# Reordering TensorE in a kernel's second listing pass, and a new order of work in its opening

The case is a two-layer decoder trunk that runs on all 8 cores of one Trainium2 chip, one sequence of the batch per core. The metric is the device time of the slowest core, in microseconds.

## The reference, cut to what matters

```python
# x: (8, 2048, 1024) float32, c: (8, 1024); DEPTH 2, D_FF 2816
def modulate(x, g, mod):
    shift, scale, gate = jnp.split(mod, 3, axis=-1)
    h = rmsnorm(x, g) * (1.0 + scale[:, None, :]) + shift[:, None, :]
    return h, gate[:, None, :]

def swiglu(h, w_in, w_out):
    g, u = jnp.split(h @ w_in, 2, axis=-1)
    return (jax.nn.silu(g) * u) @ w_out

for l in range(DEPTH):
    mod = silu(c) @ w_mod[l] + b_mod[l]             # (8, 9*1024)
    mod_f1, mod_mx, mod_f2 = jnp.split(mod, 3, axis=-1)
    h, gate = modulate(x, norm_g[l, 0], mod_f1)
    x = x + 0.5 * gate * swiglu(h, w_ffn_in[l, 0], w_ffn_out[l, 0])
    # ... token mixer (l = 0: gating and short conv; l = 1: causal pooling), then a second SwiGLU
return rmsnorm(x, final_g)
```

Before the first weight matmul the kernel needs the first two tiles of x, their norms, and the shift and scale of layer 0: 16 "rows" of 128 modulation values, each a product of 512 KB of weights with the conditioning vector.

## The kernel before

The program is a list of operations with their data dependencies. A first pass places each operation in a model of the engines' time as the code adds it. A second pass (`relist`) runs the list again in that model: the engines named in `free` take, of the operations that are ready, the one with the earliest due date; all other engines keep the order of the first pass. The order that comes out is fixed in the program: each engine is given its own list.

```python
    def relist(self, free=("dve", "act")):
        ...
            due.append(o.start + (0.0 if o.eng == "pe" else 8.0))
        # due dates are pulled earlier where a successor needs it
        ...
        fixed = {e: [] for e in self.ENGS if e not in free}     # order of the first pass
        ...
                elif e in ready:
                    _, x = heapq.heappop(ready[e])              # free engine: earliest due date
                else:
                    if at[e] >= len(fixed[e]) or not isready[fixed[e][at[e]]]:
                        continue                                # fixed engine: waits for its next
                    x = fixed[e][at[e]]
```

The opening loads six rows, two tiles of x, then the other ten rows. Chunk c (128 of the 1024 columns) needs row c (shift) and row 8 + c (scale). "Row n" below is the n-th in order of use, 2k for the shift and 2k + 1 for the scale of the k-th chunk. A row is a chain of one-column f32 matmuls or one multiply-and-sum on VectorE:

```python
    order0 = [0, 4, 1, 5, 2, 6, 3, 7]
    on_pe = (0, 2, 4, 6, 8, 10, 12, 14, 15)
    ...
            if n in on_pe:
                b = banks0.next()                               # PSUM banks 0 and 1
                for kc in range(NC):
                    add("pe", I("matmul", PS[b][:, 0:1], ap[:, kc * 128:(kc + 1) * 128], CT[:, kc:kc + 1], ...
            else:
                stt(ap, ap, 1.0, CB[:], ALU.mult, ALU.mult, ..., accum_out=M)
    ...
    for s, k in zip(range(NSLOT), (3, 5, 6, 7, 7, 7)):          # six weight slots, 1 MB read each
        load_next(s, [("MOD", 0, order0[k])])                   # slot s waits for the k-th shift row
```

A SwiGLU unit then makes seven products of four 128x128x512 matmuls (P1 to P7) from one slot. The second half of x is loaded inside the first channel mixer:

```python
    def late_x():
        for t in range(2, 4):
            add("sp", I("dma_start", out=X[:, t, :, :], ...), reads=[("A", ablk(6, 0))], ...)   # 2 MB each
    ...
                    run_segs(segs[:X_AT])
                    late_x()
                    bg_add(stats_gen([2, 3]))                   # sums of squares of the two tiles
```

Such sums of squares (`ps<-SQ,ONES` in the profile) and the pooling products of layer 1 (`ps<-CB,WMOD`) are side jobs: small groups of matmuls put between the weight matmuls (`ps<-H,SLOTS` and `ps<-ACTB,SLOTS`).

## Time and profile before

| | before |
|---|---|
| time, median of 3 runs | 1972.81 us (1972.31 to 1972.99) |
| profiled run, slowest core | 1967.0 us |
| first weight matmul, median of the cores | 58.7 us |
| cores 2 to 7 / cores 0 and 1 | 1961.1 to 1967.0 / 1938.9 and 1943.3 us |

Six cores spent 151 to 154 us at a granted clock of 0.8125, two cores none, and the two groups lie 23 us apart (means 1964.3 and 1941.1 us). I call it the limiter.

In the opening most cores are granted only 0.5, on core 0 of this run for example from 42.0 to 62.4 us; but from 38.5 to 42.0 us that core had 1.0, and there 32 one-column matmuls of the rows, all but the last two started in that time, took

```profile
38.76 3.90 PE L463 MATMUL ps<-CT,ACTB 128*128 128x1 f32 x32
```

where the same 32 take 6.83 us on core 3 in the prediction below. Start to start that is 112 ns at 1.0 and 213 ns at 0.5: a row on TensorE takes 1.8 us or 3.4 us. The records of core 3 begin only at 61.8 us; the 1.00 that the prediction's views show before it stands for missing records.

Lines with an arrow in brackets give the idle time of the engine just before that group and what ended it. The prediction below shows the views of this kernel.

### The profile page before, as it was taken

Reading aid. Unit: us, or ns where it says so; the run is one execution under the profiler, and the core shown is the slowest. Engines: PE = TensorE matmul, PEld = TensorE weight load, DVE = VectorE, ACT = ScalarE, POOL = GpSimd, SP = SyncE. Lnnn points to the kernel's source line nnn. Section 1 sums busy time; section 2 is a strip of 40 time slices with the busy share of each in tenths; the row PEclk is TensorE's granted clock in tenths of the full one; section 3 lists DMA queues with packets and bytes.
Section 4 is the critical chain, followed back from the end, with each engine's and each line's share of the span. In section 5 each row is a group of like instructions: output and inputs, shape, how many; then the busy total and the mean of one; then the engine's idle time right before and its main releaser. Section 6 shows DMA issues by size and latency. Waiting matters only on the chain.

```text
span 1967.0 us, 25441 instructions; the slowest of 8 cores (1938.9 to 1967.0 us)
## 1 busy us (share of the span) xinstructions
PE 1920.7 (98%) x8750; PEld 874.8 (44%) x8750; DVE 1695.3 (86%) x3246; ACT 1032.8 (53%) x1738; POOL 172.2 (9%) x330
## 2 busy tenths in 40 slices
PE   6999999999999999999999999999999999999997
PEld 4533444444444444444444444444444444444443
DVE  3867899999798999999988888898998889888865
ACT  4443555455564655465455545564456555574343
POOL 0000000000202000000000000000000000000000
PEclk9887899999999999999999999999999999999998
DMA  9875668786777777776755554555454444445752
GB/s 283 164 186 121 135 130 171 172 171 138 158 161 173 162 152 172 157 154 135 169 105 86 86 86 85 87 97 86 76 86 70 84 84 86 75 75 86 173 87 95
DMA packets 66653, 248.72 MB, mean 126 GB/s; under 512 B 7520, under 2 KB 7648, under 8 KB 66016
## 3 DMA queue, kind: packets, MB, share of 16 engines
q0 software_dynamic: 42192, 153.64, 47.5%
q1 hardware_dynamic: 24336, 93.45, 14.4%
q8 instruction: 74, 1.21, 0.2%
q14 instruction: 51, 0.42, 0.1%
HBM read 392.29 MB, written 8.39 MB: 204 GB/s over the span
## 4 chain that ended last, share of the span: by engine, by line
PE 91%; DMA 4%; DVE 3%; ACT 1%; SPq 0%; issue 0%; DVEq 0%; POOLq 0%
PE ps L463 91%; DMA ACTB<-wmod 2%; DMA SLOTS<-wout 2%; DVE ACTB L463 1%; DVE SLOTS L463 1%; DVE X L463 0%; DVE WMOD L463 0%; SPq L463 0%; ACT PMH L463 0%; DVE TP L463 0%; ACT ps L463 0%; DVE ps L463 0%; ACT TP L463 0%; ACT L463 0%; ACT ACTB L463 0%
## 5 line engine op out<-in xcount | busy, mean ns | idle before, releaser
L463 PE MATMUL ps<-H,SLOTS 128*128 128x512 f16 x5440 | 1215.7, 383 | 6.6 <-ACT ps L463 2.2
L463 PEld LDWEIGHTS ps<-H,SLOTS 128*128 128x128 f16 x5440 | 534.9, 99 | 668.8 <-issue 83.7
L463 ACT ACTIVATE ps<-ps 128x512 f32<-128x512 f32 x684 | 398.0, 582 | 584.8 <-PE ps L463 548.6
L463 PE MATMUL ps<-ACTB,SLOTS 128*128 128x512 f16 x2780 | 622.5, 383 | 1.4 <-DVE TP L463 0.8
L463 PEld LDWEIGHTS ps<-ACTB,SLOTS 128*128 128x128 f16 x2780 | 273.7, 99 | 337.5 <-issue 30.6
L463 DVE TENSOR_TENSOR SLOTS<-SLOTS 128x512 f16<-128x512 f16 x996 | 395.2, 418 | 17.1 <-DMA SLOTS<-wout 8.0
L463 DVE SCALAR_TENSOR_TENSOR X<-ps,GH,X 128x512 f32<-128x512 f32 x424 | 308.3, 746 | 44.6 <-PE ps L463 37.6
L463 ACT ACTIVATE TP<-ps 128x512 f32<-128x512 f32 x400 | 238.0, 595 | 130.8 <-PE ps L463 130.5
L463 DVE TENSOR_TENSOR ACTB<-TP,ps 128x512 f16<-128x512 f32 x368 | 249.3, 684 | 46.4 <-PE ps L463 27.8
L463 ACT ACTIVATE SQ<-X 128x512 bf16<-128x512 f32 x224 | 131.4, 621 | 113.1 <-DVE X L463 57.9
L463 POOL DMA_DIRECT2D SLOTS<-win x176 | 93.1, 530 | 1046.0 <-PE ps L463 974.0
L463 DVE TENSOR_TENSOR TP<-ps,TP 128x512 f32<-128x512 f32 x176 | 121.2, 688 | 65.2 <-ACT ps L463 63.4
L463 DVE SCALAR_TENSOR_TENSOR WMOD<-WMOD,CB 128x1024 f32<-128x1024 f32 x129 | 156.8, 1218 | 2.8 <-DMA WMOD<-wmod 2.6
L463 DVE TENSOR_TENSOR TP<-X,RS 128x512 f32<-128x512 f32 x192 | 129.7, 686 | 12.5 <-ACT ACTB L463 8.5
L463 DVE TENSOR_TENSOR ps<-ps,TP 128x512 f32<-128x512 f32 x176 | 122.4, 696 | 15.2 <-PE ps L463 14.0
L463 DVE TENSOR_TENSOR ACTB<-ACTB 128x1024 f16<-128x1024 f16 (+1 forms) x188 | 104.6, 566 | 1.5
L463 POOL DMA_DIRECT2D SLOTS<-wout x88 | 46.5, 528 | 521.4 <-PE ps L463 521.4
L463 ACT ACTIVATE H<-TP,MODT,AS 128x512 f16<-128x512 f32 x81 | 62.7, 805 | 20.0 <-DVE TP L463 11.9
L463 PE MATMUL ps<-SQ,ONES 128*128 128x512 bf16 x130 | 44.7, 432 | 15.0 <-DVE SQ L463 6.7
L463 ACT ACTIVATE PMH<-TP,MODT,AS 128x512 f16<-128x512 f32 x60 | 47.6, 806 | 18.1 <-DVE TP L463 18.1
L463 ACT ACTIVATE ACTB<-TP,MODT,AS 128x512 f16<-128x512 f32 x51 | 40.8, 806 | 15.4 <-PE ps L463 12.5
L463 DVE TENSOR_TENSOR SQ<-SQ 128x1024 bf16<-128x1024 bf16 (+1 forms) x56 | 36.3, 649 | 12.2 <-ACT SQ L463 11.8
(74 smaller groups left out, 562.0 us busy)
## 6 DMA issues: line engine op xcount, KB each, us to landing
SLOTS<-win POOLq DMA_DIRECT2D x176, 512.0 KB, 6.0
WMOD<-wmod SPq DMA_DIRECT2D x131, 512.0 KB, 5.8
SLOTS<-wout POOLq DMA_DIRECT2D x88, 512.0 KB, 5.4
SLOTS<-wab POOLq DMA_DIRECT2D x28, 512.0 KB, 8.7
X<-xT SPq DMA_DIRECT2D x4, 2048.0 KB, 20.8
outT<-X SPq DMA_DIRECT2D x16, 512.0 KB, 3.7
ACTB<-wmod SPq DMA_DIRECT2D x13, 512.0 KB, 25.1
CB<-cb SPq DMA_DIRECT2D x1, 512.0 KB, 5.5
```

The lines of the kernel that those rows point to most:

```text
L463: return lambda E: getattr(E, name)(*a, **k)
```

## The change

The intent: let a ready matmul on TensorE overtake a waiting one, and let the opening start sooner. Whole, without context lines:

```diff
-X_AT = 60
+X_AT = 55
+SLG = (2, 3, 4, 6, 7, 7)
...
-    order0 = [0, 4, 1, 5, 2, 6, 3, 7]
-    on_pe = (0, 2, 4, 6, 8, 10, 12, 14, 15)
+    order0 = list(range(NC))
+    on_pe = (10, 12, 14, 15)
...
                 apply_chunk(0, 0, 0, order0[j], 1, HH)
-                if j % 2 == 1:
-                    h_sums(j // 2, 1)
         apply_chunk(0, 0, 0, order0[k], 0, HH)
         apply_chunk(0, 0, 0, order0[k], 1, HH)
-        if k % 2 == 1:
-            h_sums(k // 2, 1)
+        h_sums(k - 4, 1)
...
-    for s, k in zip(range(NSLOT), (3, 5, 6, 7, 7, 7)):
+    for s, k in zip(range(NSLOT), SLG):
         load_next(s, [("MOD", 0, order0[k])])
...
-    Sd.relist()
+    Sd.relist(("dve", "act", "pe"))
```

## The prediction

> **What bounds the kernel now.** I read the page first, then the cores, then a table of stretches, then TensorE alone in the stretches that were short of matmuls, then the opening's chain of waits.
>
> The page, its busy row and two of its rows of slices:
>
> ```profile
> span 1967.0 us, 25441 instructions; the slowest of 8 cores (1938.9 to 1967.0 us)
> PE 1920.7 (98%) x8750; PEld 874.8 (44%) x8750; DVE 1695.3 (86%) x3246; ACT 1032.8 (53%) x1738; POOL 172.2 (9%) x330
> PE   6999999999999999999999999999999999999997
> PEclk9887899999999999999999999999999999999998
> ```
>
> TensorE is busy 98% of the span. Only the first and last slices are not nearly full, and the clock row dips in slices 2 to 5. So the question is where TensorE loses time, and the table of stretches says:
>
> ```profile
> 0.00:10.00 10.00, 3.62 (x9) 1.12 (x9) 1.36 (x24) 2.55 (x3) 0.19 (x4) 1.00 0.74 167
> 50.00:60.00 10.00, 9.60 (x45) 8.99 (x45) 9.21 (x26) 4.70 (x7) 2.12 (x4) 1.00 0.96 177
> 100.00:150.00 50.00, 46.14 (x176) 18.58 (x174) 33.77 (x67) 24.68 (x44) 3.54 (x7) 0.81 0.78 180
> 150.00:200.00 50.00, 47.47 (x175) 19.23 (x174) 38.50 (x74) 16.57 (x28) 2.64 (x5) 0.77 0.51 124
> 1050.00:1100.00 50.00, 50.00 (x232) 22.51 (x231) 44.41 (x83) 29.52 (x51) 4.23 (x8) 1.00 0.47 78
> ```
>
> The columns are stretch, PE, PEld, DVE, ACT, POOL busy with counts, granted clock, DMA share, GB/s. An undisturbed stretch holds 232 matmuls in 50 us, 215 ns each: that is the bound, and no change of order beats it. At a clock of 0.81 a stretch holds only 175.
>
> The losses on the slowest core, from the matmuls' start times: the first matmul of the first channel mixer starts at 59.96 us; from there to 240 us the starts are 36 us further apart in all than 216 ns each would make them, nearly all of it the clock of 0.81 and a bubble near 150 us; from 240 us to the end of the matmuls only 15.7 us, in 36 places; after the last weight matmul some 13 us remain for the final norm and the output. The change can touch the 60 us in front, the bubble, and those 15.7 us.
>
> The opening, TensorE alone:
>
> ```profile
> 39.45 6.83 PE L463 MATMUL ps<-CT,ACTB 128*128 128x1 f32 x32
> 48.38 3.55 PE L463 MATMUL ps<-CT,ACTB 128*128 128x1 f32 x16 [2.10 <-DMA ACTB<-wmod]
> 51.79 3.55 PE L463 MATMUL ps<-CT,WMOD 128*128 128x1 f32 x16
> 55.20 3.55 PE L463 MATMUL ps<-CT,ACTB 128*128 128x1 f32 x16
> 59.16 1.01 PE L463 MATMUL ps<-SQ,ONES 128*128 128x512 bf16 x2 [0.40 <-DVE AS L463]
> 59.96 2.38 PE L463 MATMUL ps<-H,SLOTS 128*128 128x512 f16 x6
> ```
>
> The opening ends in three modulation rows done on TensorE one after the other (rows 12, 14 and 15 of 16), 3.4 us from start to start, and the first of them waited for its transfer. The chain of waits names that transfer for 29.48 us, issue to landing. DMA share is 0.96 to 1.02 from 10 to 60 us: the front is a full queue and then three serial rows.
>
> The late stalls, TensorE alone again:
>
> ```profile
> 147.20 0.70 PE L463 MATMUL ps<-SQ,ONES 128*128 128x512 bf16 x2
> 149.69 0.68 PE L463 MATMUL ps<-SQ,ONES 128*128 128x512 bf16 x2 [1.80 <-DVE SQ L463]
> 152.91 1.01 PE L463 MATMUL ps<-SQ,ONES 128*128 128x512 bf16 x2 [2.53 <-DVE SQ L463]
> ...
> 1456.24 0.98 PE L463 MATMUL ps<-CB,WMOD 128*128 128x512 f16 x3 [0.85 <-DVE CB L463]
> 1483.39 0.98 PE L463 MATMUL ps<-CB,WMOD 128*128 128x512 f16 x3 [1.78 <-DVE CB L463]
> 1699.75 0.38 PE L463 MATMUL ps<-CB,WMOD 128*128 128x512 f16 x1 [0.66 <-DVE CB L463]
> ```
>
> Here TensorE stands at the head of a side job (sums of squares, pooling products) while weight matmuls of the main stream lie behind it in its fixed order. This is just what reordering TensorE in the second pass is for.
>
> **What the Trainium skill says.** "TensorE: Matmul & The Clock Gate", section "Back-to-back issue gap", gives N/2.4 + 2.5 ns for a warm matmul, 216 ns at 512 columns; this trace has 215. Its section "The HAM clock gate" says an idle window of some 3.4 us halves the clock; the records agree, one piece of 6.8 us at 0.5 follows the bubble near 150 us (the stretch from 153 to 160 us holds 21 matmuls, where 0.81 would give 27). The same section says that three busy cores of a die bring the clock to 13/16 and that it is held while the load lasts: the trace shows 0.8125 on cores 2 to 7, but only from 69 to 229 us here, under an unchanged load, and on cores 0 and 1 not at all. So I take it as a fixed cost of about 160 x (1 - 0.8125) = 30 us on the slow cores, which the change does not touch. "DMA: Bandwidth & Descriptors", section "Queues, rings and completion order", says that an engine takes turns between queues packet by packet. The trace agrees: with slot 0's load in flight (37.06 to 48.20 us, 11 us for 1 MB read) the modulation rows land 1.3 to 4.6 us apart.
>
> **The change part by part.**
>
> (1) *TensorE in the second pass.* Nothing is added or removed; a ready matmul may now overtake a waiting one, in the pass's own model of time. Movable are the stalls at side jobs: 1.80 + 2.53 near 150 us, and 0.85 + 1.78 + 0.35 + 0.66 + 0.58 from 1455 to 1705 us (the 0.35 and 0.58 are sums of squares there), together 8.55 us. The cold piece goes too if the bubble falls below a window: 6.8 us x (1 - 0.5/0.8125) = 2.6 us. Not movable: the stalls of the main stream on ACT or DVE (0.3 to 0.8 us each at 371, 979, 1025, 1227 us), where little else is ready with a free PSUM bank, and those from late weights (1.94 us at 129.76, where a load of 1 MB took 14.22 us beside the 4 MB of late input). The model knows nothing of the throttled clock and of queues in contention, so I give the reorder half of the first sum and half of the second: 4.3 + 1.3, and 1 us for pieces of the rest. That is -6.5 us, with some 4 us either way.
>
> (2) *Fewer rows on TensorE.* Nine rows become four (10, 12, 14, 15). Five times 3.4 = 17 us of TensorE go, but rows 0, 2, 4, 6 and 8 lie before 43 us, where TensorE waits for transfers anyway. VectorE gets five more products of 1.23 us and a read of 0.08, 6.5 us, three of which fall before 20 us, where it has 4.7 us of work in 10, and two at 33 to 42 us. The last three serial rows stay: worth 0.
>
> (3) *Natural chunk order.* Chunks 0 to 3 are ready first, so the first and fifth product of the first weight unit (they read only these four chunks) can run before the last rows. The banks allow about three such products ahead, because banks 0 and 1 belong to the rows: 3 x 4 x 215 ns = 2.6 us leaves the path behind 59.96 us. About 1 us of it comes back, as the next product then waits for the last chunk's apply (0.2 + 0.8 us) which these matmuls covered before: -1.6 us.
>
> (4) *Weight slots earlier.* Gates move from places (3, 5, 6, 7, 7, 7) to (2, 3, 4, 6, 7, 7). Place 2's shift row lands at 16.03 us, so slot 0 starts near 18 us instead of 37, in the middle of the first input tile, and slots 1 and 2 come near 38 and 42 us instead of 49 and 53. Before the last row landed (50.91 us), 1 MB and a third of slots were read; now it is 2 to 2.5 MB. At 330 GB/s the extra 1 MB is 3 us of later rows, hence of later serial rows: +3 us, less if the gates in practice fall later. Early slots win nothing by themselves; no stall between 60 and 73 us names them.
>
> (5) *X_AT 60 to 55.* The late input waits for the result of weight unit 6 in both versions; its issue at 114.81 us follows that result at 114.05. So the transfer doesn't move; only the statistics of those tiles become due 5 segments (5 x 1.05 us) sooner. Worth 0, perhaps a worse stall.
>
> Sum: -6.5 - 1.6 + 3 = about -5 us. A change of this kind is usually kept because it won a little, and the opening may fill better than I can see by hand, so I lean to -7.5: 1972.8 - 7.5 = 1965.
>
> **The rivals.** *The opening gains for real*: if the slots take less from the rows than I fear, and TensorE runs main matmuls from about 45 us, all of 3 to 7 us comes off in front, and the sum is -13, 1960 us. For it: the last rows wait for a queue that the slots share today also. Against: banks 0 and 1 and the other four chunks hold back the rest. *The transfers collide*: rows land 5 us later, the statistics stall longer because the order is rigid on the chip and the model lands the late input too early; the sum is +3, 1976 us. For it: DMA share is at 1.0 in the opening. *The reorder wins nothing*: its model has no gap where the chip has one, so the order stays as it was; 1971 us. *The throttle moves*: if the steadier start keeps six cores out of the 0.81 state as cores 0 and 1 are now, 30 us more fall, near 1935; nothing in the change aims at it. If the throttle lasts longer, the kernel gets slower by as much.
>
> **Range and chances.** Opening -5 to +5, body -12 to -1: 1953 to 1975 holds it 8 times in 10. Two per cent is 39 us, over twice all stalls that the change can reach, so only the throttle gives faster (0.03) or slower (0.01) by that much; within 2%: 0.96.
>
> **What would show it.** Right: the stalls before side jobs at 150, 1456, 1483 and 1700 us shrink or vanish and the matmuls from 240 us on lose under 12 us in place of 15.7; some 12 weight matmuls stand before the last rows; the last row lands 2 to 5 us later; the 0.81 stretch is again about 160 us. Wrong: the main stream starts without a break before 50 us; rows land as before; new stalls on transfers or PSUM copies take the place of the old; or cores 2 to 7 are not throttled. Should the sums from 1455 to 1705 us stay, step (1) fails. Should the rows land no later, step (4) fails.

## More of the kernel before

A difference under 2% counts as "same".

The profiled run, 1968.5 us in all, was 4 us faster than the three timed ones, of which no trace is kept.

## The result

The changed kernel took 1965.81 us, median of 4 runs (1964.78 to 1966.27). The kernel before had 1972.81 us over its three fast runs; a fourth, of 2149.87 us, was slow and is left out. The ratio of the fast runs is 0.9964, interval 0.9945 to 0.9984; a ratio is the mean time of one kernel's fast runs over that of the other's of the same rounds, so it is not quite the ratio of the medians. By the 2% rule it is "same"; by the interval a small gain.

The page of the profiled run, and the stretches that answer to those shown of before (same columns):

```profile
span 1964.7 us, 25319 instructions; the slowest of 8 cores (1929.0 to 1964.7 us)
PE   2999999999999999999999999999999999999997
PEclk6888889999999999999999999999999999999999
```

```profile
100.00:150.00 50.00, 45.77 (x190) 19.54 (x188) 37.05 (x76) 26.90 (x49) 3.17 (x6) 0.88 0.90 209
150.00:200.00 50.00, 50.00 (x192) 20.71 (x191) 41.48 (x80) 20.91 (x32) 3.69 (x7) 0.81 0.56 117
```

The page looks as before but for its edges: the first slice holds less TensorE work (2 tenths for 6, as five rows have gone), and the lower clock ends later. The stretch from 150 us on is now full (192 matmuls at 0.81, before 175), the stretch before it still has a hole. TensorE alone from 120 us, with lines left out, shows both:

```profile
119.76 2.32 PE L464 MATMUL ps<-H,SLOTS 128*128 128x512 f16 x10
126.31 10.80 PE L464 MATMUL ps<-H,SLOTS 128*128 128x512 f16 x37 [4.23 <-DVE TP L464]
136.94 0.70 PE L464 MATMUL ps<-SQ,ONES 128*128 128x512 bf16 x2
...
146.66 0.70 PE L464 MATMUL ps<-SQ,ONES 128*128 128x512 bf16 x2
147.18 0.70 PE L464 MATMUL ps<-ACTB,SLOTS 128*128 128x512 f16 x2
147.70 0.44 PE L464 MATMUL ps<-H,SLOTS 128*128 128x512 f16 x1
```

The sums of squares carry no wait any more, and after 146 us matmuls of two main streams alternate in ones and twos: that is the new order filling gaps. The hole at 122 us is a main-stream wait and has grown from 1.94 to 4.23 us on the slowest cores. These were not at the same clock there: the slowest core of before was already at 0.8125, this one still at 1.0. On cores without the limiter the hole was 2.6 and 4.6 us before and is 2.9 and 3.7 us after, so there it has not grown. The total of TensorE's waits shows the same; columns are total, times, longest. Before:

```profile
PE ps L463 <- DVE SQ L463: 6.7, 4, 2.5
PE ps L463 <- DVE CB L463: 3.3, 3, 1.8
```

After:

```profile
PE ps L464 <- DVE SQ L464: 1.8, 1, 1.8
PE ps L464 <- DVE CB L464: 0.3, 1, 0.3
```

The one wait for sums of squares that is left is the last of the program, with nothing behind it. The opening, TensorE alone:

```profile
50.27 3.54 PE L464 MATMUL ps<-CT,ACTB 128*128 128x1 f32 x16 [5.26 <-DMA ACTB<-wmod]
54.11 3.54 PE L464 MATMUL ps<-CT,WMOD 128*128 128x1 f32 x16 [0.30 <-DMA WMOD<-wmod]
57.51 3.55 PE L464 MATMUL ps<-CT,ACTB 128*128 128x1 f32 x16
60.92 0.59 PE L464 MATMUL ps<-SQ,ONES 128*128 128x512 bf16 x1
61.30 1.06 PE L464 MATMUL ps<-H,SLOTS 128*128 128x512 f16 x2
```

Rows 12, 14 and 15 end the opening as before, each starting later (50.27 for 48.38), and no weight matmul stands ahead of them. All three run at a granted clock of 0.5, which lasts here from 42.3 to 66.2 us. At 1.0 the three in series would take some 5 us less (3 x 1.6, an estimate from the 112 and 213 ns above); no run tried to keep the clock up in the opening.

I add the losses up over cores. A stall is here a start-to-start time over 215.5 ns, divided by the granted clock where that was lower, by more than 50 ns, between the first and the last weight matmul; side stalls are those before a side job. In every run the traces of two cores lack some 30 matmul records, mostly of sums of squares; a gap of just one matmul before such a sum is taken for a missing record and not counted.

| means | before, throttled cores (2 to 7) | after, throttled (0, 1, 4 to 7) | before, free (0, 1) | after, free (2, 3) |
|---|---|---|---|---|
| first weight matmul, us | 58.9 | 61.3 | 59.1 | 61.6 |
| stalls, us | 21.4 | 13.9 | 23.7 | 12.9 |
| of these side stalls | 10.0 | 0.5 | 11.1 | 0.9 |
| time lost to 0.8125, us | 26.6 | 28.8 | 0 | 0 |
| span, us | 1964.3 | 1961.6 | 1941.1 | 1931.2 |

So 7 to 11 us of stalls are gone; the side stalls fell by 9.5 to 10.2 us, and on throttled cores main stalls rose by 2.1. The first weight matmul came 2.5 us later; and on throttled cores the limiter took 2.2 us more. It began at 69 us before and at 135 to 137 us after. Which pair of cores escapes differs from run to run.

This account is of the two profiled runs. They differ by 2.7 us in mean span on throttled cores and by 9.9 us on free ones, the timed medians by 7.0. What the timed runs of before lost beyond the profiled one no trace shows; a limiter that began later in them, with the stalls outside it, would fit but is not shown.

### The profile page after: what moved, and what is told of

It is laid out like the page before. It is cut to its first block, busy times and chain, and to the rows that moved or that the text cites. A ratio compares the mean times of both kernels' runs of the same rounds, so it can differ in the third digit from the quotient of the medians.

```text
span 1964.7 us, 25319 instructions; the slowest of 8 cores (1929.0 to 1964.7 us)
## 1 busy us (share of the span) xinstructions
PE 1905.0 (97%) x8670; PEld 858.9 (44%) x8670; DVE 1697.3 (86%) x3256; ACT 1031.1 (52%) x1738; POOL 172.2 (9%) x330
## 4 chain that ended last, share of the span: by engine, by line
PE 89%; DMA 4%; DVE 3%; ACT 2%; SPq 1%; issue 0%; POOL 0%; DVEq 0%; POOLq 0%
PE ps L464 89%; DMA WMOD<-wmod 2%; DMA SLOTS<-win 1%; SPq L464 1%; DMA SLOTS<-wout 1%; DVE WMOD L464 1%; DVE X L464 1%; DVE ACTB L464 1%; DVE SLOTS L464 0%; DVE TP L464 0%; ACT PMH L464 0%; ACT ps L464 0%; ACT TP L464 0%; ACT L464 0%; ACT ACTB L464 0%
## 6 DMA issues: line engine op xcount, KB each, us to landing
ACTB<-wmod SPq DMA_DIRECT2D x13, 512.0 KB, 28.8
```

## The experiments

**Theory**: the gain is the reorder alone, at the side jobs; the opening costs time, because early slots take the queue from the last rows, and three rows in series on TensorE end it. **Rivals**: the opening or the earlier late input gives the gain; the difference is the limiter's phase.

The jobs ran on other chips, whose limiter differs so much (0 to 224 us lost per core) that times compare badly across chips. So I also give, for each profiled run, the mean over the 8 cores of the *span without the limiter*: the span less what each matmul at a granted 0.8125 took over 215.5 ns (at most 50 ns for one). It compares runs of one chip only, since a slowed TensorE also hides stalls. For the first pair it is 1938.5 us before and 1932.4 after (the record does not say whether these two profiles are of one chip).

The "336th weight matmul" of the expectations is the 336th of `ps<-H,SLOTS` alone, the median of the cores. It marks the end of the stretch with the hole and the late sums of squares. A free TensorE may put other weight matmuls before it, so between a fixed and a free order it is a rough mark.

### Chip B: the two halves of the change, and two undone parts

Before, timed beside these four: median 2150.74 us. All cores were throttled for 1045 us or more.

**reorder_alone**

```diff
# the kernel before
-    Sd.relist()
+    Sd.relist(("dve", "act", "pe"))
```

> The kernel before with nothing but TensorE added to the second listing pass. Theory (the reorder is what wins): the waits of TensorE near 150, 1456, 1483 and 1700 us vanish, stalls of the middle fall from some 22 us to about 15 on the throttled cores, the first weight matmul stays at 58 to 60 us, and the time falls by about 7 us or more (1963 to 1966). Rival (the win comes with the opening or with the earlier late input): within 2 us of before.

Measured: 2141.4 us median, ratio 0.9959 (0.9927 to 0.9991), without the limiter 1922.0 us; first weight matmul 57.0 us, sooner than the 58 to 60 expected; side stalls 0.3 us. TensorE's waits have no line for pooling products at all, and one for sums of squares, the last:

```profile
PE ps L463 <- DVE TP L463: 2.9, 1, 2.9
PE ps L463 <- DVE SQ L463: 1.8, 1, 1.8
```

The wait for "TP" is the hole near 122 us, which the reorder does not touch.

**opening_alone**

```diff
# the changed kernel
-    Sd.relist(("dve", "act", "pe"))
+    Sd.relist()
```

> The changed kernel with TensorE's order left fixed in the second pass: new opening, new slot gates, X_AT 55. Theory (the opening costs a little): the first weight matmul at about 61 us, stalls of the middle as before (some 22 us), time 0 to 4 us above before. Rival (the opening gives the gain): below before by 3 us or more.

Measured: 2151.14 us median, ratio 1.0006 (0.9983 to 1.0029), without the limiter 1935.4 us, 13.4 above the run before it; first weight matmul 61.9 us; side stalls 10.3 us. TensorE alone, lines left out:

```profile
135.47 0.59 PE L464 MATMUL ps<-SQ,ONES 128*128 128x512 bf16 x2 [1.48 <-DVE SQ L464]
...
148.24 1.01 PE L464 MATMUL ps<-SQ,ONES 128*128 128x512 bf16 x2 [3.36 <-DVE SQ L464]
151.64 0.58 PE L464 MATMUL ps<-SQ,ONES 128*128 128x512 bf16 x1 [2.39 <-DVE SQ L464]
```

With TensorE's order fixed the side stalls are back, and no gain is seen (the interval leaves room for 3.7 us of gain and 6.2 us of loss). The two runs settle the first question: the gain is the reorder.

**old_slot_gates**

```diff
# the changed kernel
-SLG = (2, 3, 4, 6, 7, 7)
+SLG = (3, 5, 6, 7, 7, 7)
```

> The changed kernel with the slot gates of before. Theory (early slots take the queue from the last rows): the last modulation row lands 2 to 4 us earlier than in the changed kernel (55.7 us), the first weight matmul comes near 58.5 us, and the time is 2 to 3 us below the changed kernel. Rival (the rows' landing does not matter, or the early weights save something later): no earlier first matmul, or a new wait for weights in the first units that gives it back.

Measured: 2142.76 us median, ratio 0.9964 (0.9930 to 0.9997); without the limiter 1918.5 us, the lowest of this chip. The last row landed at 51.6 us (median of the cores; 55.8 in the changed kernel), and the first weight matmul came at 55.7 us, 5.8 below the changed kernel's in its first profile:

```profile
48.53 3.55 PE L464 MATMUL ps<-CT,WMOD 128*128 128x1 f32 x16
52.94 3.54 PE L464 MATMUL ps<-CT,ACTB 128*128 128x1 f32 x16 [0.86 <-DMA ACTB<-wmod]
56.35 0.59 PE L464 MATMUL ps<-SQ,ONES 128*128 128x512 bf16 x1
56.73 1.06 PE L464 MATMUL ps<-H,SLOTS 128*128 128x512 f16 x2
58.01 22.31 PE L464 MATMUL ps<-H,SLOTS 128*128 128x512 f16 x83
```

From 58 us on 83 matmuls run without a break, so on this core no wait for the later slots shows. By the clock on the wall the gain over reorder_alone does not show: the runs of one kernel spread over up to 18 us here. The changed kernel itself, which is one edit away, was not run on this chip; chip C has that pair, on top of the split input.

**rows_on_dve**

```diff
# the changed kernel
-    on_pe = (10, 12, 14, 15)
+    on_pe = ()
```

> The changed kernel with no modulation row on TensorE, all 16 on VectorE. Theory (the last three rows in series on TensorE end the opening): a row takes 1.3 us on VectorE in place of 3.4, so the first weight matmul comes about 2 to 3 us after the last landing, near 58 us, 3 us below the changed kernel. Rival (VectorE becomes the bound of the opening, with 4 more products of 1.3 us beside the applies): the first weight matmul at 61 us or later, time same or longer.

Measured: 2143.28 us median, ratio 0.9964 (0.9928 to 1.0), without the limiter 1920.6 us. Neither theory nor rival had this form:

```profile
43.22 2.60 PE L464 MATMUL ps<-H,SLOTS 128*128 128x512 f16 x4 [4.10 <-ACT H L464]
54.61 2.72 PE L464 MATMUL ps<-H,SLOTS 128*128 128x512 f16 x6 [8.80 <-ACT ps L464]
58.10 1.01 PE L464 MATMUL ps<-H,SLOTS 128*128 128x512 f16 x2 [0.76 <-ACT ps L464]
...
66.10 14.20 PE L464 MATMUL ps<-H,SLOTS 128*128 128x512 f16 x57 [0.24 <-DVE ps L464]
```

Four weight matmuls did run ahead of the last rows, but TensorE then waited 8.8 us and was continuous only from 66 us. Its 30th weight matmul came at 66.2 us. The changed kernel, of the same slot gates, has its 30th at 70.2 us in the first profile and at 69.6 and 70.1 us on chips C and D, opening_alone at 70.1 us on this chip: some 4 us later. So the series of rows on TensorE did hold the opening back, as the theory said, though the first matmul is no measure of it here. The four early matmuls themselves are under 1 us of that. old_slot_gates, with its rows on TensorE but later slots, has the 30th at 64.6 us.

### Chip C: the late input

On this chip die 1 of many runs was at another clock than die 0, so almost every timed run counts as slow. The profiled run of before_again is fast, those of the other three are slow. So their times are not compared. I use the waits, the loads and the span without the limiter, and where a point rests on this chip alone I say so.

**before_again** (the kernel before, unchanged)

> The kernel before, unchanged, for a trace of it on the same chip as the runs beside it. All theories: first weight matmul near 58.7 us, the 336th near 158 us, stalls before sums of squares near 150 us and before pooling products later.

Measured: two runs, 2192.34 us (slow) and 2101.98 us, the profiled one; first weight matmul 58.4 us, 336th 155.2; side stalls 8.4 us, before the same side jobs as in the first profile.

**after_again** (the changed kernel, unchanged)

> The changed kernel, unchanged, on the same chip. Theory (reorder wins 7 us, opening gives back 2 to 3): first weight matmul near 61.4 us, the 336th near 148 us, 4 to 8 us below before. Rival (the difference of the first measurement came from the limiter's phase): within 2 us of before.

Measured: 2087.6 us median against 2103.3, slow runs; first weight matmul 61.0 us, 336th 149.0; side stalls 0.6 us. Without the limiter 1927.3 us against 1933.2 for before_again: 5.9, as 6.1 in the first pair.

**late_x_split**

```diff
# the changed kernel
-    def late_x():
-        for t in range(2, 4):
-            add("sp", I("dma_start", out=X[:, t, :, :], ...), reads=[("A", ablk(6, 0))], ..., nbytes=128 * 16384)
+    def late_x(n):
+        t, c0 = 2 + n // 2, 4 * (n % 2)
+        add("sp", I("dma_start", out=X[:, t, c0:c0 + 4, :], ...), reads=[("A", ablk(6 + n, 0))], ..., nbytes=128 * 8192)
...
-                    run_segs(segs[:X_AT])
-                    late_x()
-                    bg_add(stats_gen([2, 3]))
+                    # late_x(n) after segment X_AT + 7 n, n = 0 to 3; statistics of tile 2 after n = 1, of tile 3 after n = 3
```

> The changed kernel with the late input in four pieces of 1 MB, each released by the next weight unit (6, 7, 8, 9), and its statistics in two parts. Theory (the remaining bubble near 122 us comes from one weight load taking 14.9 us beside 4 MB of input on the other queue): weight loads there take 6 to 10 us, the wait of 4.2 us at 122 us falls below 1 us, no piece at half clock follows, the 336th matmul comes 4 us or more sooner than in the changed kernel. Rival (VectorE is late there for another reason): the wait stays.

Measured: 2103.61 us median, all runs slow; the 336th weight matmul at 146.1 us, 2.9 sooner than after_again (4 expected); without the limiter 1924.4 us, also 2.9 less. Transfers from 100 to 145 us with the median from issue to landing at the end of the line, after_again:

```profile
X<-xT SPq DMA_DIRECT2D x2, 2048.0 KB, 18.8
SLOTS<-wout POOLq DMA_DIRECT2D x5, 512.0 KB, 14.1
```

late_x_split:

```profile
X<-xT SPq DMA_DIRECT2D x4, 1024.0 KB, 11.8
SLOTS<-wout POOLq DMA_DIRECT2D x5, 512.0 KB, 11.2
```

TensorE of after_again, then of late_x_split:

```profile
117.56 9.80 PE L464 MATMUL ps<-H,SLOTS 128*128 128x512 f16 x41
129.15 6.20 PE L464 MATMUL ps<-H,SLOTS 128*128 128x512 f16 x18 [1.78 <-DVE TP L464]
```

```profile
117.63 15.32 PE L464 MATMUL ps<-H,SLOTS 128*128 128x512 f16 x62
```

The wait is gone: between 120 and 132 us after_again has a main-stream stall of 0.5 to 3.4 us on every core, late_x_split none above 0.7. The piece at half clock that goes with it on three cores of after_again comes on none here. So the wait did come from the late input; this rests on slow runs of this chip. The loads fell only to 11.2 us, not to the 6 to 10 that I wrote; there is enough lead at that.

**split_and_old_gates** (both edits)

> The late input in four pieces and the slot gates of before, the rest as in the changed kernel. If both theories hold the gains add: first weight matmul near 55.7 us, no wait at 122 us, 336th matmul near 141 us, some 8 us below the changed kernel in undisturbed time; less where the clock limiter takes it back. Rival (one gain covers the other): no better than the better of the two.

Measured: first weight matmul 55.5 us, 336th 141.8, without the limiter 1919.0 us: 5.4 below late_x_split and 8.3 below after_again; 2095.68 us median, all slow. So the old gates still win on top of the split input. Whether each is worth as much alone on this chip was not run, so that the gains simply add is not shown.

### Chip D: three checks and the best version

Here whole runs passed without the limiter. Fast runs fall into two groups: with one piece of some 160 us at 0.8125 on a pair of cores, or without. Before: 1972.24 to 1972.42 us (3 runs) and 1945.83 to 1950.07 (6 runs). I compare within a group.

**after_third** (the changed kernel, unchanged)

> The changed kernel unchanged, for the comparison on this chip. As recorded before: first weight matmul 61 us, last row landing 55 to 56 us, 336th weight matmul 148 to 149 us, 0.3 to 0.4% below before if fast runs are to be had.

Measured: with a limiter piece 1965.67 and 1966.34 us, 6.3 below before; without 1937.88 and 1939.79, 9.3 below before's mean of 1948.2. The ratio over both groups, 0.9977 (0.9881 to 1.0072), mixes them. Its profiled run had no limiter: mean span 1933.2 us, first weight matmul 61.6.

**nine_rows**

```diff
# the changed kernel
-    on_pe = (10, 12, 14, 15)
+    on_pe = (0, 2, 4, 6, 8, 10, 12, 14, 15)
```

> The changed kernel with nine modulation rows on TensorE as before (0, 2, 4, 6, 8, 10, 12, 14, 15). Theory (fewer rows on TensorE are worth nothing, since the early rows lie in waits for transfers): first weight matmul within 1 us of the changed kernel's on the same chip, 336th within 2 us. Rival (the five rows matter, or cost VectorE): first matmul 2 us or more later (or earlier).

Measured, in one run: first weight matmul 63.7 us (after_third 61.6), 336th 149.9 (after_third 145.9), mean span 1935.2 us, 2.0 above after_third. The rival is right. The reason is in the second line:

```profile
48.96 3.54 PE L464 MATMUL ps<-CT,ACTB 128*128 128x1 f32 x16 [1.20 <-DMA ACTB<-wmod]
56.36 3.54 PE L464 MATMUL ps<-CT,WMOD 128*128 128x1 f32 x16 [3.86 <-DMA WMOD<-wmod]
59.76 3.55 PE L464 MATMUL ps<-CT,ACTB 128*128 128x1 f32 x16
```

The last four rows are loaded into the buffers of rows 0 to 3, when these are used up. Row 0 on TensorE is used up after row 1 on VectorE, and so on: the last transfers were issued in the order 13, 12, 15, 14 here, and 12, 13, 14, 15 in the changed kernel. Row 14, for which TensorE waits, was issued at 30.09 and landed at 56.23 us (27.23 and 54.20 in after_third).

**x_at_60**

```diff
-X_AT = 55
+X_AT = 60
```

> The changed kernel with X_AT 60. Theory (the transfer waits for weight unit 6 either way): the late input is issued at the same place, right after unit 6's result (109.9 us in the changed kernel), and the 336th weight matmul comes within 2 us. Rival (the earlier statistics are part of the gain): sums of squares stall TensorE again near 140 to 150 us, or the 336th matmul comes 3 us or more later.

Measured, in one run: the late input issued at 110.3 us (median of the cores; after_third 109.6), 0.26 us after the same weight load in both; 336th weight matmul 146.8 us; span without the limiter 1932.0 us. Worth nothing, as expected; a limiter piece on one pair of cores makes up this run's 1963.29 us.

**best**

```diff
# late_x_split and
-SLG = (2, 3, 4, 6, 7, 7)
+SLG = (3, 5, 6, 7, 7, 7)
-    on_pe = (10, 12, 14, 15)
+    on_pe = (10, 12, 14)
```

> The changed kernel with slot gates of before, the late input in four pieces, and row 15 on VectorE (rows 10, 12, 14 stay on TensorE). If the series of rows is what ends the opening: first weight matmul 2 us sooner than with old gates alone (55.7 us), near 53.5 us; no wait near 122 us; span without the limiter 10 us below the changed kernel. Rival (VectorE is as late with row 15): first matmul near 55.7 us or a wait of TensorE right after it.

Measured: the fast runs took 1928.85 to 1930.07 us, all without a limiter piece; before without one had 1948.2, the changed kernel 1938.8. That is 1.0% below before in the same group. Two of its six runs were slow (2083.53 and 2085.49 us). The ratio over all fast runs, 0.9859 (0.9772 to 0.9946, recorded as "unclear"), flatters it, since before's three throttled runs are in it. Mean span 1923.0 us, 10.2 below after_third, 10 expected. This is three edits at once: what row 15 is worth of it no pair of runs on one chip shows.

```profile
48.48 3.55 PE L464 MATMUL ps<-CT,WMOD 128*128 128x1 f32 x16
52.37 0.59 PE L464 MATMUL ps<-SQ,ONES 128*128 128x512 bf16 x1 [0.34 <-DVE MODT L464]
52.75 1.91 PE L464 MATMUL ps<-H,SLOTS 128*128 128x512 f16 x4
55.33 2.85 PE L464 MATMUL ps<-H,SLOTS 128*128 128x512 f16 x10 [0.67 <-DVE SLOTS L464]
58.79 2.38 PE L464 MATMUL ps<-H,SLOTS 128*128 128x512 f16 x9 [0.62 <-ACT H L464]
```

The first weight matmul is at 52.4 us (median), 3 us sooner than with row 15 on TensorE, but the lines after it have waits that end with work of VectorE or ScalarE. At the 30th weight matmul 1.0 us of the 3 is left (63.2 us for 64.2 in split_and_old_gates, on chip C). So theory and rival are each half right. The wait near 122 us, which the expectation had gone, is small but there (0.65 us on the slowest core at 123.42 us, up to 1.7 on another), and with the split sums of squares a side stall came back: 1.63 us at 130.17 us, side stalls 1.9 us in all.

## Why the prediction was right, point by point

The time was 1965 us predicted and 1965.81 measured, inside the range. That it was hit within a microsecond is luck. The steps sum to 5 us less (1968); the other 2.5 us were added because such changes are usually kept, which is no mechanism; and the steps were less exact than their sum. Of the signs that the prediction named, the stalls at the side jobs vanished, the matmuls from 240 us on lose 11.2 us on the slowest core (under 12 expected, 15.7 before), and the last row landed 4.8 us later there; the twelve weight matmuls ahead of the last rows did not come.

1. *Reorder, -6.5 us*. Right in mechanism and place: side stalls fell from 10.0 to 0.5 us on throttled cores, and with TensorE's order fixed (opening_alone) they are 10.3 us. I halved the term out of doubt in the listing pass's model; in truth nearly all of it came, and the stalls in all fell by 7.4 us on throttled and 10.8 us on free cores. What I called not movable stayed: main stalls were 11.3 us before and 13.4 after on throttled cores, 12.6 and 12.0 on free ones. The piece at half clock, for which I took off 1.3 us, did not go on most cores but moved: on the slowest it lasts 6.8 us again, from 124.2 us, in and after the hole.
2. *Fewer rows on TensorE, 0*. Wrong by 2 us (nine_rows against after_third, one run). I looked at TensorE's waits only, and not at when each row's buffer comes free for a later row.
3. *Natural order, -1.6 us*. Not borne out: no weight matmul ran ahead of the last rows. In the listing pass's model slot 0 lands after all rows, as that model serves transfers one after another (the kernel's own pass, run again, has the last row at 44.9 us and slot 0 at 48.2); on the chip it landed at 33.45 us, ahead of rows 6 to 15. That this is the reason is argued, not tested by a run. No run isolates the natural order either, so its own worth stays open.
4. *Early slots, +3 us*. Right in mechanism, too small: undoing them alone brought the first weight matmul from 61.1 to 55.5 us (chip C, both with the split input), 5.5 us, of which the span without the limiter kept 5.4; both runs are slow ones, but the fast run old_slot_gates on chip B has its first matmul at 55.7 us too. The last row landed 4 us sooner, and the series of rows on TensorE followed it. The mis-sized part is the bytes: I let 2 to 2.5 MB of slots be read before the last row, but slots 0 to 2, 3 MB, had landed by 52.69 us on the slowest core, ahead of row 15 at 55.73; the 1.7 MB more than before are 5 us at the prediction's 330 GB/s (an estimate).
5. *X_AT, 0*. Right.

The opening in all came out as +2.5 us at the first weight matmul, for +1.4 predicted; as the reorder alone brings that matmul to 57.0 us (chip B), the new opening costs more than the 2.5 us show. Those misses cancelled against step 1. One point the prediction had as fixed moved: in the profiled runs the limiter cost the throttled cores 28.8 us for 26.6, so part of the gain was given back there. The free cores show the change's own worth, 10 us, by one pair of cores each and by the unthrottled runs on chip D (9.3 us).

Two readings in the prediction do not hold. The 175 matmuls of 150 to 200 us are not what a clock of 0.81 allows: a bubble lies in that stretch, and the full stretch after the change holds 192. And the half-clock piece near 150 us agrees with the idle window of some 3.4 us in the Trainium skill's "TensorE: Matmul & The Clock Gate", section "The HAM clock gate", only loosely: no idle stretch there is longer than 2.53 us, and in the 3.4 us before the piece began at 150.6 us TensorE was busy for 1.4.

## What to carry to other kernels

When an engine works through a fixed list, look for its waits at the head of small side jobs while main work stands ready behind: they are what a reorder can win, and here it won nearly all of them. Starting a transfer early is not free when the queue is full and what ends the stage is still behind it: here 1 MB slots loaded before they were needed cost 5.5 us at the first weight matmul. Split a large transfer over several releases when a stream of loads with short lead runs beside it, and check the granted clock of each core before a difference below 2% is explained.

## What the Trainium skill lacked or had wrong

- "TensorE: Matmul & The Clock Gate", section "The HAM clock gate": it has a whole die at 13/16 once three cores run dense matmuls, held while the load lasts. With eight cores loaded alike the first pair and x_at_60 show one stretch of some 160 us and none in the 1650 us after it, on some pairs of cores and not on the others of the same die (cores 0 and 1 against 2 and 3); no piece at all on eight cores (after_third, best); and on chip B repeated pieces, 15.1 us each but one on core 4 and 1186 us in all there (reorder_alone). Some slow runs come near what the page says: in one of before on chip D (2327.05 us) cores 0 to 3 have a mean clock of 0.815 to 0.821. What decides between these is open.
- The same page, section "Back-to-back issue gap": some 60 cycles for 1 to 64 columns. The one-column f32 products here start 112 ns apart at a granted clock of 1.0 and 213 ns at 0.5, in two matmuls per call, and their weight loads take 192 and 333 ns where the page's section "LDWEIGHTS (loading the stationary operand)" would give 107 for 128 columns (an estimate from its formula). The page gives no time for f32.
- "DMA: Bandwidth & Descriptors", section "Queues, rings and completion order": rows that land during a slot's load fit its turns between queues (no run here shows the packet as the unit), but no page gives what a load gets beside another queue. Here 1 MB read took 5.4 to 6.0 us as the median over the run for the SwiGLU weights, 11 us beside modulation rows and 14.1 us beside 4 MB of input.
